# The planned cost of the first loads and of one addition of squares in a self-ordering decoder layer kernel

## The chip, the cores and the metric

One NeuronCore of a Trainium2 chip runs the kernel. Its engines work side by side, each through its own list of instructions in order: TensorE (PE, with its weight loads as PEld), VectorE (DVE), ScalarE (ACT), GpSimd (POOL), and SyncE (SP), which issues most of the DMAs. An instruction that has to wait for another engine or for a load holds everything behind it on its own engine. The metric is the device time of one execution in microseconds (us); less is better.

## The reference

One layer on a sequence of 1024 tokens and 1024 channels, all in f32. Cut to what matters here:

```python
mod = silu(c) @ mod_w + mod_b
shift, scale, gate = split(mod, 3)
h = rmsnorm(x, norm_g) * (1.0 + scale) + shift
u = h @ w_in                       # 5 x 1024 columns: cv, cg, cs, lx, ls
v = cv * sigmoid(cg)               # then a causal convolution of 31 taps,
...                                # LayerNorm, silu, @ pw2_w, times silu(cs)
...                                # lx: short convolution, gates, linear scan, times silu(ls)
x = x + (1.0 + gate) * (concat(conv, lru) @ w_out)
out = rmsnorm(x, final_g)
```

## The kernel before

**Layout.** Everything is kept transposed: channels on the 128 partitions, tokens along the free dimension, in two halves of 512 (`START`). The input x is eight k tiles `x0` to `x7` of 128 x 1024. A product of f32 quality is made of three matmuls in a faster format, from a high part (the value rounded to that format) and a low part (what the rounding left): high x high, high x low, low x high. So every operand of TensorE is first split: ScalarE casts or scales to the high part, VectorE subtracts to the low part.

**The opening.** TensorE should start before the RMS norm and the shift are known. So the first four column tiles (`FIRST`) are computed from x times a scale column alone; the norm's factor per token (`rbc`) and the shift's contribution (`bias`) are applied to the results later. For k tile k this needs:

- the scale column `gs[k]`: a dot product of a 128 x 1024 tile of `mod_w` (`modw8` is for k = 0, `modw9` for k = 1 and so on) with the conditioning row `sc`, on VectorE (`dot`, with an accumulator), and a small operation that makes `gs` from it;
- the high part `uh` and the low part `ul` of x times `gs`, each per half of the tokens: `uh` on ScalarE (the first half of k = 0 on VectorE), `ul` on VectorE;
- the split of the weights, `fhi` on ScalarE and `flo` on VectorE (the names' numbers go by pairs: `flo0` holds k = 0 and 1, `flo2` holds k = 2 and 3);
- 21 matmuls of 512 columns into the banks `first...`: 4 column tiles x 3 terms for the first half and 3 x 3 for the second; the fourth column tile's second half is made up later (`late`).

Beside this run the squares of x (`sq`, ScalarE) and their additions into one tile (VectorE), whose column sums give `rbc`: TensorE sums them (`token_stats`), a small row is written to memory (`rrowd`) and read back as a broadcast to all partitions. Then come the shift's dot products (`modw0` to `modw7`), sums `fsum` of weights times shift, the three slots `NEXT` computed from the same unshifted operands (slots 4 to 6), the `bias` column sums (`psbias`), the gating products `v`, and the operands with the shift in them (`uh`, `ul` written anew) for slot 7 and all that follow.

**What sets the order.** No engine's list is written by hand. Each operation is recorded with an engine, a cost in us, a priority (smaller is sooner) and what it reads and writes. `Plan.order` then plays the whole kernel through with these costs: whenever an engine is free by its model, it takes the ready operation with the smallest priority, and that becomes the engine's order. A load counts as landed when the modelled queue has moved it at its cost. `slack` adds us to the readiness of an operation that hangs on another engine. The real machine then runs these lists in order, with real waits. So a cost in the model moves no time by itself; it moves instructions.

The loads of the opening are recorded in the order of `LOADS`, priority -100, -99, -98 and so on: `s` is the scale's tile of `mod_w`, `a` and `b` the halves of x0, `w` or `W` weights, `x` the later tiles of x, `h` the shift's tiles. The lines that matter are 382 to 385 (`DMA`, the cost of a load), 872 to 878 (the low part and its slack) and 897 to 903 (squares and their additions).

Of the kernel before, what the change touches and what calls it, by code (L numbers as in the profile page):

```python
# [12 lines left out]
ALU = mybir.AluOpType  # L13
# [4 lines left out]
KT = D // P  # L18
# [23 lines left out]
SUM = ("DVE", "DVE", "DVE", "DVE", "DVE", "DVE", "DVE", "DVE")  # L42
# [41 lines left out]
SCALE = ("DVE", "DVE", "DVE", "DVE", "DVE", "DVE", "DVE", "DVE")  # L84
SQP, RSP, BIP, HHP, HCH, EVP = -84, -110, -50, -56, 0.1, -80
RBC_LAG = 2.0


LOADS = "s0 a0 w0 s1 b0 w1 x1 W2 s2 x2 s3 x3 W4 s4 x4 s5 x5 W6 s6 x6 s7 x7 h0 h1 h2 h3 h4 h5 h6 h7".split()
# [205 lines left out]
def hymba_layer(ctx: ExitStack, tc: tile.TileContext, xT, vecs, mod_w, w_first, w_in,  # L295
# [3 lines left out]
    act, dve, pool, pe, sp = nc.scalar, nc.vector, nc.gpsimd, nc.tensor, nc.sync  # L299
# [19 lines left out]
    S = Plan(pools)  # L319
# [41 lines left out]
    def TT(prio, eng, out, a, b, op, n=T, r=(), w=(), reserve=0, after=()):  # L361
        e = dve if eng == "DVE" else pool
        return S.op(eng, d_cost(n) if eng == "DVE" else p_cost(n),
                    lambda: e.tensor_tensor(out=out(), in0=a(), in1=b(), op=op), prio, r, w,  # L364
                    reserve=reserve, lock=not in_psum(r), after=after)
# [14 lines left out]
                    lock=not in_psum(r))  # L380

    def DMA(prio, out, in_, nbytes, r=(), w=(), after=(), reserve=0):
        return S.op("SP", max(0.1, nbytes / 360e3),
                    lambda: sp.dma_start(out(), in_()), prio, r, w, after=after,
                    reserve=reserve)

    def store(prio, eng, out, in_, r, nbytes):
# [359 lines left out]
    for i in range(IDLE):  # L747
        if i == IDLE0:
            for z in (0, 1):
# [3 lines left out]
             after=[spread_op] if i >= IDLE0 else [])  # L753
# [34 lines left out]
    for i, ld in enumerate(LOADS):  # L788
        p = due[ld] = i - 100.0
        k = int(ld[1])  # L790
# [4 lines left out]
        elif ld[0] in "wW":  # L795
# [5 lines left out]
                w=keys(rw))  # L801
            for j in range(k, k + nk):
# [4 lines left out]
                if j:  # L807
                    SUB(p, "DVE", fw_part(lo, j), fw_part(rw, j), fw_part(hi, j), FW,
                        r=[(rw, jj), (hi, jj)], w=[(lo, jj)])
# [31 lines left out]
                    [("a0", 0), ("b1", 0)], [("b1", 0)], lock=True)  # L841

    a0 = ctile("a0", 1)
    begun, uhs, uls, scaled, split_u, last_u = {}, [], [], [], [], {}
    for k in range(KT):
        p = due[f"s{k}"]
        a_ = col(macc, KT + k)
        if k == 0:
            first_dot(p)
        else:  # L850
            dot(SCALE[k], p - 1.5 * (k == 1), KT + k, [gs_op, *(split_u[:1] if k == 1 else [])])
        gs_op = S.op("DVE", 0.2, lambda k=k, a_=a_: dve.scalar_tensor_tensor(
            out=col(gs, k), in0=a_, scalar=col(b1, k), in1=vec("norm_g", k), op0=ALU.add,
            op1=ALU.mult), p, [("macc", KT + k), ("b1", 0)], [("gs", k)], lock=True)
        p = max(p, due[f"x{k}"] if k else p, due[f"w{k}"])
        uh, ul = big_buf(f"uh{k}", F32R, 4), big_buf(f"ul{k}", F32R, 4)
        uhs.append(uh)
        uls.append(ul)
        x_, g = xt[k], gs[:, k:k + 1]
        for a, e in START if k < UK else ((0, T),):  # L860
            n = e - a
            hk = halves(x_, a, e)
            if k == 0 == a:
                o = TS(p, part(uh, a, e), part(x_, a, e), g, None, ALU.mult, n=n,
                       r=hk + [("gs", k)], w=halves(uh, a, e))
            else:
                o = ACT(p, part(uh, a, e), part(x_, a, e), AF.Copy, n, scale=g,
                        r=hk + [("gs", k)], w=halves(uh, a, e))
            if k == 0 == a:
                rw, hi, lo = fw[0]  # L870
                SUB(p, "DVE", fw_part(lo, 0), fw_part(rw, 0), fw_part(hi, 0), FW,
                    r=[(rw, 0), (hi, 0), *halves(uh, a, e)], w=[(lo, 0)])
            split_u.append(STT(
                p, part(ul, a, e), part(x_, a, e), g,
                lambda uh=uh, a=a, e=e: uh()[:, a:e].bitcast(F32), ALU.mult, ALU.subtract, n,
                r=hk + halves(uh, a, e) + [("gs", k)], w=halves(ul, a, e)))
            if k == 0 < a:
                split_u[-1].slack = 1.0
        scaled.append(o)
        for z in range(3 if k == 0 else 0):  # L880
            for i, ps in enumerate(psf):
                o = fw_mm(p, ps, i, uh, ul, k, START[:1], z=z)
                if z == 0:
                    begun[i, 0] = o
                last_u[k, i, 0] = o
        for ch, (a, e) in enumerate(START):
            for i, ps in enumerate(psf):
                if (a, e) not in cuts[i] or k == 0 == a:
                    continue
                q = p + 0.1 * ch if k < LASTK else due[f"w{KT - 1}"] + 0.01 * ((i + 1) % 4) + 0.001 * ch  # L890
                for z in range(3) if k < ZK else (None,):
                    o = fw_mm(q + 0.003 * (z or 0), ps, i, uh, ul, k, ((a, e),),
                              after=[begun[i, a // H]] if k == 0 and a % H else [], z=z)
                last_u[k, i, ch] = o

    sqs = []
    for k in range(KT):
        p = SQP + k
        sq = big_buf(f"sq{k}")
        ACT(p, sq, xt[k], AF.Square, r=[xt[k]], w=[sq], after=[scaled[k]])  # L900
        if k:
            to = sqs[0]
            TT(p, SUM[k], to, to, sq, ALU.add, r=[to, sq], w=[to])
        else:
            sqs.append(sq)
    rbc = big_buf("rbc", parts=4)
# [14 lines left out]
    def turn():  # L921
# [6 lines left out]
        r=[("rrowd", 0)], w=[rbc])  # L928
# [637 lines left out]
```

## Time and profile before

| what | value |
|---|---|
| median of three runs | 732.12 us (731.79 to 732.23) |
| the profiled execution, its own time | 732.15 us |
| its span, first to last instruction | 730.4 us |
| mean granted TensorE clock | 0.997 |

The profile is of one execution. A row of its timeline has the start in us, the duration in us, engine and line, the operation, what it writes `<-` what it reads (without buffer numbers) and how many were merged; in brackets the idle time of the engine just before, and what ended it. A row of the chain has start, duration and what; the chain is followed back from the last instruction to what released each step. A row of a stretch has, for a window of time, the busy time and number of instructions of PE, PEld, DVE, ACT and POOL, the granted clock, the DMA engines' busy share and GB/s. Matmuls overlap in a pipeline, so their rate is read from start to start.

### The profile page before, as it was taken

The numbers are of one execution on the slowest core, as the hardware profiler recorded it, in microseconds if no ns is written. First come the engines' busy times: TensorE is split into PE (matmuls) and PEld (weight loads), VectorE is DVE, ScalarE is ACT, GpSimd is POOL, SyncE is SP. The second block draws the span as 40 slices with busy tenths as digits, with TensorE's granted clock in tenths as the row PEclk, the third lists the DMA queues.
The fourth block names the chain that finished last, engine by engine and source line by source line (L and its number), as shares of the span: only waits on it lengthen the run. The fifth ranks groups of instructions, "written<-read, shape, count | busy, mean of one in ns | idle before, by whom it ended". The sixth has DMA issues, their size and how long they took to land.

```text
span 730.4 us, 8922 instructions
## 1 busy us (share of the span) xinstructions
PE 721.1 (99%) x3270; PEld 599.7 (82%) x3270; DVE 637.5 (87%) x912; ACT 461.1 (63%) x620; POOL 97.9 (13%) x107
## 2 busy tenths in 40 slices
PE   8999999999999999999999999999999999999996
PEld 7888888888888888888888888888888888887885
DVE  6998999999989987688899995998999657899647
ACT  5760585876877977957867896835754334657421
POOL 0034012031222332133121100000000000000001
PEclk9999999999999999999999999999999999999998
DMA  8972023388599799799884536244233430622306
GB/s 321 407 245 90 1 75 91 101 189 200 131 256 238 156 210 212 159 206 213 196 177 90 112 85 190 95 165 165 104 107 115 174 116 0 230 83 92 116 1 230
DMA packets 37499, 112.11 MB, mean 153 GB/s; under 512 B 4168, under 2 KB 12880, under 8 KB 37456
## 3 DMA queue, kind: packets, MB, share of 16 engines
q1 hardware_dynamic: 24048, 76.50, 29.9%
q0 software_dynamic: 12528, 34.26, 26.0%
q10 hardware_dynamic: 880, 0.79, 0.3%
q8 instruction: 25, 0.41, 0.2%
q14 instruction: 18, 0.15, 0.1%
HBM read 64.69 MB, written 12.59 MB: 106 GB/s over the span
## 4 chain that ended last, share of the span: by engine, by line
PE 96%; DVE 2%; DMA 1%; ACT 0%; SPq 0%; issue 0%; DVEq 0%; ACTq 0%
PE ps L495 66%; PE first L775 5%; PE papw L606 3%; PE pbpw L606 3%; PE gate L1197 3%; PE pupw L606 3%; PE puout L606 2%; PE paout L606 2%; PE out L676 2%; PE pcpw L606 1%; PE pb0out L606 1%; PE pcout L606 1%; DVE o L356 1%; DMA x<-in_xT_dram 1%; PE late L775 1%; PE out6b L676 1%
## 5 line engine op out<-in xcount | busy, mean ns | idle before, releaser
L495 PE MATMUL ps<-uh,whi 128*128 128x512 f32 x576 | 224.4, 390 | 0.0
L495 PE MATMUL ps<-uh,wlo 128*128 128x512 f32 x576 | 224.3, 389 | 0.0
L495 PE MATMUL ps<-ul,whi 128*128 128x512 f32 x576 | 224.3, 389 | 0.0
L495 PEld LDWEIGHTS ps<-uh,whi 128*128 128x128 f32 x576 | 108.2, 188 | 22.5
L495 PEld LDWEIGHTS ps<-ul,whi 128*128 128x128 f32 x576 | 108.2, 188 | 22.4
L495 PEld LDWEIGHTS ps<-uh,wlo 128*128 128x128 f32 x576 | 108.1, 188 | 22.3
L337 ACT CAST whi<-raw 128x1024 fp32r<-128x1024 f32 x46 | 48.0, 1047 | 33.9 <-PE ps L495 32.8
L345 ACT ACT_TABLE_LOAD x48 | 61.6, 1283 | 6.2 <-DVE sp8h L378 2.8
L369 POOL DMA_DIRECT2D es<-cq x45 | 40.3, 908 | 156.9 <-ACT cq L345 115.6
L364 DVE TENSOR_TENSOR wlo<-raw,whi 128x1024 fp32r<-128x1024 f32 x39 | 47.5, 1219 | 13.6 <-ACT whi L337 13.6
L356 DVE SCALAR_TENSOR_TENSOR cacc<-v,V,cacc 128x511 f32<-128x511 f32 (+14 forms) x75 | 55.6, 741 | 0.5
L356 DVE SCALAR_TENSOR_TENSOR caccs<-v,V,caccs 128x511 f32<-128x511 f32 (+6 forms) x70 | 52.1, 744 | 2.3 <-ACT caccs L345 1.0
L356 DVE SCALAR_TENSOR_TENSOR caccs<-c,wsum,caccs 128x511 f32<-128x511 f32 (+6 forms) x70 | 52.0, 743 | 0.6
L369 POOL DMA_DIRECT2D oo<-co x42 | 38.3, 913 | 92.1 <-ACT co L345 36.7
L495 PE MATMUL ps<-yh,wlo 128*128 128x512 f32 x128 | 49.8, 389 | 0.0
L495 PE MATMUL ps<-yl,whi 128*128 128x512 f32 x128 | 49.8, 389 | 0.0
L495 PE MATMUL ps<-yh,whi 128*128 128x512 f32 x128 | 49.8, 389 | 0.0
L364 POOL TENSOR_TENSOR o<-fin,bc 128x256 f32<-128x256 f32 x4 | 2.9, 730 | 282.6 <-DMA out_dram<-o 277.5
L356 DVE SCALAR_TENSOR_TENSOR xs<-ps,V,xs 128x512 f32<-128x512 f32 (+3 forms) x48 | 35.8, 745 | 0.2
L345 ACT ACTIVATE cq<-v,V 128x511 f32<-128x511 f32 (+14 forms) x45 | 31.9, 708 | 0.0
L364 POOL TENSOR_TENSOR wlo<-raw,whi 128x1024 fp32r<-128x1024 f32 x7 | 18.2, 2627 | 88.8 <-ACT whi L337 88.8
L356 DVE SCALAR_TENSOR_TENSOR modw<-modw,sc 128x1024 f32<-128x1024 f32 x23 | 30.1, 1313 | 0.0
(380 smaller groups left out, 1455.7 us busy)
## 6 DMA issues: line engine op xcount, KB each, us to landing
raw<-in_w_in_dram SPq DMA_DIRECT2D x36, 512.0 KB, 5.2
modw<-in_mod_w_dram SPq DMA_DIRECT2D x24, 512.0 KB, 8.6
raw<-in_w_out_dram SPq DMA_DIRECT2D x10, 512.0 KB, 3.9
scsd<-scs SPq DMA_DIRECT2D x8, 512.0 KB, 4.3
acc<-in_xT_dram SPq DMA_DIRECT2D x8, 512.0 KB, 4.2
accd<-acc SPq DMA_DIRECT2D x8, 512.0 KB, 2.7
rawpw<-in_pw_dram SPq DMA_DIRECT2D x8, 512.0 KB, 3.4
scsr<-scsd SPq DMA_DIRECT2D x8, 512.0 KB, 5.4
```

The costliest lines, as they stand in the source:

```text
L337: act.copy(out(), in_())
L345: act.activation(out=out(), in_=in_(), func=func, **kw)
L356: dve.scalar_tensor_tensor(out=out(), in0=in0(), scalar=scalar, in1=in1(), op0=op0, op1=op1, accum_out=accum)
L364: lambda: e.tensor_tensor(out=out(), in0=a(), in1=b(), op=op), prio, r, w,
L369: return S.op("POOL", ISSUE, lambda: pool.dma_start(out(), a(), accum_op=ALU.add), prio, r, w, lag=RATE * n / T, after=after)
L495: pe.matmul(part(ps, a - off, b - off)(), k3(lhs)()[:, k, :], rhs[k]()[:, a:b], start=(k == 0 and lhs is wh and rhs is xh and (a - off) % ...
L606: pe.matmul(part(ps, 0, c1 - c0)(), half(*lhs)()[:, j * P:j * P + P], half(*rhs)()[:, c0:c1], start=start and j == 0 and z == 0, stop=j == ...
L676: pe.matmul(part(ps, a - off, e - off)(), k3(lhs)()[:, k, :], rhs()[:, i * H + a % H:i * H + a % H + e - a], start=k == KORD[0] and lhs is ...
L775: pe.matmul(part(ps, a - off, b - off)(), fw_part(lhs, k, i * P, i * P + P)(), rhs()[:, a:b], start=k == 0 and lhs is wh and rhs is xh, st ...
L1197: pe.matmul(ps(), lhs()[:, j, :], rhs()[:, c0:c1], start=st == 0, stop=st == 2)
```

## The change

Four numbers of the plan and one dependence. Loads of the opening are costed at 410 thousand bytes per us instead of 360 thousand (those with a priority below -68.1, which are all of `LOADS`); the second and third load, the first half of x0 and the weights of k = 0, get costs of their own, 2.27 and 1.2 us; the slack of the low part of k = 0's second half goes from 1.0 to 0.5 us; and the addition of tile 1's squares waits for the low part of tile 2.

```diff
+FIRSTCOST, EARLYRATE, SQD, SQK, ULS = {-99: 2.27, -98: 1.2}, 410e3, 1, 1, 0.5
...
     def DMA(prio, out, in_, nbytes, r=(), w=(), after=(), reserve=0):
-        return S.op("SP", max(0.1, nbytes / 360e3),
-                    lambda: sp.dma_start(out(), in_()), prio, r, w, after=after,
+        cost = max(0.1, nbytes / (EARLYRATE if prio < -94.5 + KT * 3.3 else 360e3))
+        cost = FIRSTCOST.get(round(prio), cost) if prio < -96 else cost
+        return S.op("SP", cost, lambda: sp.dma_start(out(), in_()), prio, r, w, after=after,
                     reserve=reserve)
...
-    begun, uhs, uls, scaled, split_u, last_u = {}, [], [], [], [], {}
+    begun, uhs, uls, scaled, split_u, last_u, last_split = {}, [], [], [], [], {}, []
...
             if k == 0 < a:
-                split_u[-1].slack = 1.0
+                split_u[-1].slack = ULS
         scaled.append(o)
+        last_split.append(split_u[-1])
...
             to = sqs[0]
-            TT(p, SUM[k], to, to, sq, ALU.add, r=[to, sq], w=[to])
+            TT(p, SUM[k], to, to, sq, ALU.add, r=[to, sq], w=[to],
+               after=[last_split[k + SQD]] if k <= SQK else [])
```

What it does to the lists shows at three places. The numbers in the names are those of buffers.

**VectorE, k tiles 0 and 1.** Before, from the first high part on (`ul0` is the low part of k = 0, `modw9` the dot product for k = 1):

```order
L378 TENSOR_SCALAR uh0_170<-x0_125,gs_90 128x512
L364 TENSOR_TENSOR flo0_176<-fraw0_140,fhi0_155 128x512
L356 SCALAR_TENSOR_TENSOR ul0_186<-x0_125,gs_90,uh0_170 128x512
L364 TENSOR_TENSOR flo0_176<-fraw0_140,fhi0_155 128x512
L356 SCALAR_TENSOR_TENSOR modw9_142,macc_93<-modw9_142,sc_152 128x1024
L356 SCALAR_TENSOR_TENSOR ul0_186<-x0_125,gs_90,uh0_170 128x512
L852 SCALAR_TENSOR_TENSOR gs_90<-macc_93,b1_94,V_77 128x1
L364 TENSOR_TENSOR flo2_223<-fraw2_166,fhi2_215 128x512
L356 SCALAR_TENSOR_TENSOR ul1_229<-x1_159,gs_90,uh1_220 128x512 x2
```

And now:

```order
L379 TENSOR_SCALAR uh0_164<-x0_125,gs_90 128x512
L357 SCALAR_TENSOR_TENSOR ul0_173<-x0_125,gs_90,uh0_164 128x512
L365 TENSOR_TENSOR flo0_181<-fraw0_132,fhi0_167 128x512
L357 SCALAR_TENSOR_TENSOR modw9_148,macc_93<-modw9_148,sc_151 128x1024
L854 SCALAR_TENSOR_TENSOR gs_90<-macc_93,b1_94,V_77 128x1
L357 SCALAR_TENSOR_TENSOR ul0_173<-x0_125,gs_90,uh0_164 128x512
L365 TENSOR_TENSOR flo0_181<-fraw0_132,fhi0_167 128x512
L357 SCALAR_TENSOR_TENSOR ul1_220<-x1_171,gs_90,uh1_211 128x512 x2
```

The dot product and the scale column of k = 1 and the second low part of k = 0 stand ahead of the low weights of k = 1 (the second `flo0`); the first low part stands ahead of the low weights of k = 0; the low weights of k = 2 went behind the low parts of k = 1. On ScalarE the second copy of the row `sc` went ahead of the cast `fhi0` of k = 0, and the high parts of k = 1 ahead of the cast of k = 2's weights.

**VectorE, k tiles 2 and 3.** Before, from tile 2's dot product (`modw10`) on:

```order
L356 SCALAR_TENSOR_TENSOR modw10_182,macc_93<-modw10_182,sc_152 128x1024
L364 TENSOR_TENSOR flo2_223<-fraw2_166,fhi2_215 128x512
L852 SCALAR_TENSOR_TENSOR gs_90<-macc_93,b1_94,V_77 128x1
L364 TENSOR_TENSOR sq0_192<-sq0_192,sq1_239 128x1024
L356 SCALAR_TENSOR_TENSOR ul2_269<-x2_200,gs_90,uh2_260 128x512 x2
L356 SCALAR_TENSOR_TENSOR modw11_212,macc_93<-modw11_212,sc_152 128x1024
L364 TENSOR_TENSOR flo4_291<-fraw4_244,fhi4_284 128x512
L852 SCALAR_TENSOR_TENSOR gs_90<-macc_93,b1_94,V_77 128x1
```

And now:

```order
L357 SCALAR_TENSOR_TENSOR modw10_191,macc_93<-modw10_191,sc_151 128x1024
L365 TENSOR_TENSOR flo2_234<-fraw2_179,fhi2_224 128x512
L854 SCALAR_TENSOR_TENSOR gs_90<-macc_93,b1_94,V_77 128x1
L357 SCALAR_TENSOR_TENSOR modw11_218,macc_93<-modw11_218,sc_151 128x1024
L357 SCALAR_TENSOR_TENSOR ul2_269<-x2_204,gs_90,uh2_257 128x512 x2
L854 SCALAR_TENSOR_TENSOR gs_90<-macc_93,b1_94,V_77 128x1
L365 TENSOR_TENSOR sq0_199<-sq0_199,sq1_237 128x1024
L365 TENSOR_TENSOR flo4_296<-fraw4_245,fhi4_283 128x512
```

The dot product of tile 3 (`modw11`) stands ahead of tile 2's low parts (`ul2`), the addition of squares behind them.

**SP and ScalarE, around the broadcast of the row statistics.** SP's loads before:

```order
L384 DMA raw8_499<-in_w_in_dram 128x1024
L384 DMA raw6_502<-in_w_in_dram 128x1024
L384 DMA graw1_518<-in_gate_w_dram 128x256
L384 DMA rbc_528<-rrowd_101 128x1024
L384 DMA modw6_564<-in_mod_w_dram 128x1024
```

And now:

```order
L386 DMA raw8_478<-in_w_in_dram 128x1024
L386 DMA graw1_490<-in_gate_w_dram 128x256
L386 DMA modw5_516<-in_mod_w_dram 128x1024
L386 DMA rbc_539<-rrowd_101 128x1024
L386 DMA modw6_566<-in_mod_w_dram 128x1024
```

The load of `modw5` (the shift's sixth tile) went from ahead of the slots' weights to just ahead of the broadcast load. On ScalarE, whose list issues the write of the small row, stood before:

```order
L345 ACTIVATE st_100<-token_stats_121,eps_t_88 128x8
L337 CAST whi4_512<-raw4_455 128x1024
L345 ACTIVATE fsum_486<-raw5_465,shift_91 128x128
L337 COPY rbc_528<-token_stats_121 8x128
L337 CAST ghi0_530<-graw0_477 128x256
L926 DMA rrowd_101<-rbc_528 8x128
```

And now:

```order
L346 ACTIVATE st_100<-token_stats_121,eps_t_88 128x8
L338 CAST whi4_521<-raw4_430 128x1024
L338 CAST whi7_529<-raw7_469 128x1024
L338 COPY rbc_539<-token_stats_121 8x128
L338 CAST whi8_541<-raw8_478 128x1024
L930 DMA rrowd_101<-rbc_539 8x128
```

Two casts of whole weight tiles stand where two smaller operations stood. Among TensorE's matmuls the bias sums (`psbias`) went 18 matmuls back, from inside slot 6 to the beginning of slot 7, and the sums of the squares (`token_stats`) 3 matmuls back. From about a quarter of each list on, the orders of before and now are equal, apart from buffer numbers.

## The prediction

> **What bounds the kernel now.** I read the page first (busy shares), then the waits of TensorE, then the engines' busy time by stretch, and last the opening instruction by instruction. Of the page:
>
> ```profile
> PE 721.1 (99%) x3270; PEld 599.7 (82%) x3270; DVE 637.5 (87%) x912; ACT 461.1 (63%) x620; POOL 97.9 (13%) x107
> ```
>
> TensorE is busy for 99% of the span, so an edit to the order pays only where TensorE stands still. The view of its waits names those places (total us, times, longest):
>
> ```profile
> PE first L775 <- DVE ul L356: 0.8, 1, 0.8
> PE puout L606 <- ACT eout L337: 0.7, 1, 0.7
> ```
>
> The second lies near 661 us. The first is in the opening, as this stretch shows (us of each engine, then clock, DMA share, GB/s):
>
> ```profile
> 10.00:15.00 5.00, 4.25 (x19) 2.95 (x18) 3.62 (x7) 3.88 (x6) 0.00 (x0) 1.00 1.03 420
> ```
>
> TensorE (first) has holes there, and VectorE (third) 1.4 us of idle time. The timeline shows the holes, and the chain the undisturbed pace (start, us, what):
>
> ```profile
> 8.62 1.19 PE L775 MATMUL first<-uh,fhi 128*128 128x512 f32 x4 [0.22 <-ACT fhi L337]
> 9.65 1.08 PE L775 MATMUL first<-uh,flo 128*128 128x512 f32 x4
> 13.75 0.98 PE L775 MATMUL first<-ul,fhi 128*128 128x512 f32 x3 [0.75 <-DVE ul L356]
> 14.64 1.20 PE L775 MATMUL first<-uh,fhi 128*128 128x512 f32 x4
> 15.67 1.08 PE L775 MATMUL first<-uh,flo 128*128 128x512 f32 x4
> 24.75 0.46 PE L775 MATMUL first<-ul,fhi 128*128 128x512 f32 x1
> 25.05 0.40 PE L775 MATMUL first<-uh,fhi 128*128 128x512 f32 x1
> 47.82 2.96 PE first L775 x12
> 56.21 29.92 PE ps L495 x132
> ```
>
> The pace is 29.92 / 132 = 0.227 us for a 512-column matmul. A k tile has 21 of them (4 column tiles of the first half and 3 of the second, three terms each): 4.76 us. Tile 0 begins at 8.62 and tile 1 at 14.64. The first four from 8.62 take until 9.65, 1.03 instead of 0.91, so a start from rest costs 0.12. Without a hole tile 1 would start at 8.62 + 4.76 + 0.12 = 13.50. **Lost there: 1.14.** Tile 1 starts from rest again (14.64 to 15.67, 1.03): **0.12**. At 24.75 the low part of tile 3 comes just in time, and from it to the next matmul are 0.30: **0.07**. All that an opening can give back at these places is 1.14 + 0.12 + 0.07 = 1.33.
>
> **Why the hole is there.** VectorE and ScalarE in the same stretch, and the landings that they need (for tile 1's scale weights, its x and tile 3's scale weights the issue, then us from issue to landing):
>
> ```profile
> 8.60 0.69 DVE L364 TENSOR_TENSOR flo<-fraw,fhi 128x512 fp32r<-128x512 f32 x1 [0.70 <-ACT fhi L337]
> 9.21 0.75 DVE L356 SCALAR_TENSOR_TENSOR ul<-x,gs,uh 128x512 fp32r<-128x512 f32 x1
> 11.19 0.69 DVE L364 TENSOR_TENSOR flo<-fraw,fhi 128x512 fp32r<-128x512 f32 x1 [1.24 <-ACT fhi L337]
> 11.80 1.22 DVE L356 SCALAR_TENSOR_TENSOR modw<-modw,sc 128x1024 f32<-128x1024 f32 x1
> 12.95 0.75 DVE L356 SCALAR_TENSOR_TENSOR ul<-x,gs,uh 128x512 fp32r<-128x512 f32 x1
> 13.61 0.21 DVE L852 SCALAR_TENSOR_TENSOR gs<-macc,b,V 128x1 f32<-128x1 f32 x1
> 14.62 1.41 DVE L356 SCALAR_TENSOR_TENSOR ul<-x,gs,uh 128x512 fp32r<-128x512 f32 x2 [0.19 <-ACT uh L345]
> 9.93 0.72 ACT L345 ACTIVATE uh<-x,gs 128x512 fp32r<-128x512 f32 x1 [0.87 <-DMA x<-in_xT_dram]
> 10.56 0.60 ACT L337 CAST fhi<-fraw 128x512 fp32r<-128x512 f32 x1
> 11.07 1.05 ACT L345 ACTIVATE sq<-x 128x1024 f32<-128x1024 f32 x1
> 13.86 1.34 ACT L345 ACTIVATE uh<-x,gs 128x512 fp32r<-128x512 f32 x2 [0.15 <-DVE gs L852]
> L384 SPq DMA_DIRECT2D modw<-in_mod_w_dram x1: 432/432/432, 2.6 to 2.6; - x1
> DMA to landing us min/median/max: 6.6/6.6/6.6
> L384 SPq DMA_DIRECT2D x<-in_xT_dram x1: 710/710/710, 4.0 to 4.0; - x1
> DMA to landing us min/median/max: 7.8/7.8/7.8
> L384 SPq DMA_DIRECT2D modw<-in_mod_w_dram x1: 328/328/328, 7.9 to 7.9; - x1
> DMA to landing us min/median/max: 9.0/9.0/9.0
> ```
>
> VectorE works in order. After the low part of tile 0's first half (9.21) the next in its queue is tile 1's low weights, whose cast ends at 11.16: it stands 1.24 us, while the scale weights of tile 1 have been there since 2.6 + 6.6 = 9.2 and the high part of x0's second half since 10.65. Both stand behind the waiting instruction, and TensorE behind them.
>
> **The change, part by part.** It alters planned costs only, so nothing is added or removed; what counts is the new order. I go through it with the durations above; on VectorE an independent successor starts about 0.08 before the end (8.60 + 0.69 against 9.21), a dependent one 0.04 to 0.05 after it.
>
> *Tile 0.* The first low part goes ahead of tile 0's low weights, into the 0.70 that VectorE waited for the cast (7.90 to 8.60); being 0.75 long it hardly delays the low weights, which run 8.62 to 9.31, and TensorE wants them at 9.65. Free. The second copy of the conditioning row goes ahead of that cast on ScalarE, into time in which it waited for the load: free; if it were late it would cost its 0.58, as it would then hold the cast and the first matmul.
>
> *Tile 1.* The dot product with the scale weights starts at 9.23 (landed 9.2) and ends at 10.45; the scale column is ready at 10.70; the low part of the second half follows, 10.71 to 11.46, and TensorE wants it at 8.62 + 0.12 + 18 x 0.227 = 12.83: 1.4 early. Tile 1's low weights run 11.37 to 12.06. ScalarE ends the squares at 12.12 and then, with the column there and x1 landed at 4.0 + 7.8 = 11.8, makes tile 1's high parts, 12.07 to 13.41; the first is done at 12.79, and TensorE wants it at 13.50: 0.7 early. Low parts 12.83 to 14.24, wanted from 13.50 + 8 x 0.227 = 15.32. So tile 1 can start at 13.50.
>
> *Tile 2.* Low weights, dot product and low weights of tile 3 run 14.16 to 16.5, the column is there at 16.7, the high part at 17.5; wanted at 13.50 + 4.76 = 18.26: 0.7 early. Now the dot product for tile 3 stands ahead of tile 2's low parts, and it waits for its weights, landed 7.9 + 9.0 = 16.9. Behind it queue those low parts: 18.10 to 18.85 for the first, wanted at 18.26 + 1.82 = 20.08: 1.2 early. If that load were later by more than 1.2, every further us would be TensorE's.
>
> *Tile 3.* One addition of squares (1.22, by the equal dot product) now stands behind tile 2's low parts instead of ahead of them. Column, addition and low weights put tile 3's low parts at 21.3; the first is done at 22.05, wanted at 18.26 + 4.76 + 0.45 = 23.47. The narrow place at 24.75 gets 1.4 of cover. Later tiles gain more, as VectorE stays some 0.8 ahead of its old times while landings stay as they were: the loads' order on SP is unchanged up to the eighth x tile, and DMA is full at 420 GB/s either way.
>
> So 1.33 comes back. What of it is kept? TensorE then has no hole until 661 us, so all later work moves up by this much, if the rest keeps pace. From about 165 us on the orders of before and after are equal, so the 0.7 near 661 and the end stay as they are.
>
> *Further on.* The load that broadcasts the row statistics stands one 512 KB load further back on SP, and two casts of 1.05 stand ahead of it on ScalarE. VectorE waits for it at 54 us, has idle time again between 60 and 70, and is then full until TensorE's slot 7 takes its low parts one by one, from 90 us on (columns of the stretches as above; the cast is a group of the page):
>
> ```profile
> L337 ACT CAST whi<-raw 128x1024 fp32r<-128x1024 f32 x46 | 48.0, 1047 | 33.9 <-PE ps L495 32.8
> 54.05 3.68 DVE L364 TENSOR_TENSOR first_u<-first,rbc 128x512 f32<-128x512 f32 x6 [1.75 <-DMA rbc<-rrowd]
> 60.00:65.00 5.00, 5.00 (x24) 4.15 (x23) 3.31 (x8) 0.00 (x0) 2.11 (x1) 1.00 0.32 105
> 65.00:70.00 5.00, 5.00 (x24) 4.14 (x23) 4.17 (x13) 0.00 (x0) 0.11 (x1) 1.00 0.00 0
> 80.00:85.00 5.00, 5.00 (x24) 4.15 (x23) 5.00 (x11) 3.08 (x6) 0.00 (x0) 1.00 0.00 0
> ```
>
> So VectorE can fall back by 1.69 + 0.83 = 2.5 against TensorE at no cost. The inserted load takes between 1.25 (512 KB at the 420 GB/s of the opening) and a whole flight of 6.6, the casts between 0 and 2.1 (they replace two smaller operations): together 1.25 to 8.7. I take 1.25 + 1.05 = 2.3, near the lower end because queued loads followed each other at that rate in the opening. That is just covered: zero.
>
> The bias sums move 18 matmuls back among TensorE's work, and sigmoids and the gating products `v` hang on them:
>
> ```profile
> 87.62 0.17 ACT L337 COPY bias<-psbias 128x7 f32<-128x7 f32 x1 [0.73 <-PE psbias L962]
> 89.73 2.19 ACT L345 ACTIVATE first_u<-first_u,bias 128x1024 f32<-128x1024 f32 x2
> 91.19 2.91 DVE L356 SCALAR_TENSOR_TENSOR v<-first_u,bias,first_u 128x512 f32<-128x512 f32 x4
> ```
>
> The copy comes at 87.62 + 18 x 0.227 - 1.33 = 90.4. An activation between it and the sigmoids is gone, so the first of these starts some 1.4 later instead of 2.1 and ends at 92.9. VectorE has three more operations of 0.66 ahead of the first product and reaches it between 91.19 + 2.0 - 1.33 = 91.9 and, if it gains nothing, 93.2. It waits 0 to 1.0 there, and low parts queue behind; by the 2.3 above it is at the later end, so again zero.
>
> Sum: 732.15 (the profiled execution's own time: span 730.4 and 1.75 around it) - 1.33 = 730.8. That execution is 0.03 above the median of the three runs, 732.12.
>
> **The rivals.** *The broadcast holds VectorE (slower).* If the inserted load delays the broadcast by a whole flight, VectorE falls back by 6.6, 2.5 of it is covered, and TensorE waits 4.1 in slot 7: 732.15 - 1.33 + 4.1 = 734.9; with the casts in full on top, 737.0. It decides from 2.5 on, and from 3.8 on the kernel is slower than before. For it: VectorE is full from 70 us on, and my value is close to the cover. Against: loads in the opening stood behind each other in the queue (flights of 6.6 to 9.0) and still came at 420 GB/s. With both casts in full and the load at 1.3 it would be 3.4, less 2.5: 0.9 lost, 731.7.
>
> *The end loses it to the clock.* The end is sparse; a stretch and a piece of the chain:
>
> ```profile
> 722.00:725.00 3.00, 2.08 (x16) 1.70 (x15) 2.20 (x8) 0.63 (x2) 0.32 (x1) 1.00 0.67 221
> 722.98 0.72 PE finbc L705 x4
> ```
>
> The granted clock is still 1.00 with 2.08 busy of 3. If work that comes 1.33 sooner met a half clock, this piece would double: 730.8 + 0.7 = 731.5. [...] The three executions of before lie within 0.44 (731.79 to 732.23), so a 0.7 of this kind is rare.
>
> *The cover in the opening is thinner.* Tile 1's and tile 2's high parts have 0.7 each. Were they late by 0.7 more than that, half of the gain would go: 731.5.
>
> *More than the sum.* In the chain the 12 matmuls from 47.82 took 2.96 instead of 2.72, a start from rest after the row statistics that is not in my sum. If it went too, with such a term or two more, it would be 0.3 to 0.5: 730.4.
>
> *The change does nothing here.* If the wait only moved to the next load, the result would be 732.1. Against it: the load that matters landed at 9.2, 2.6 before VectorE used it.
>
> **How the numbers follow.** 0.2% of 732.12 is 1.46, about what a measurement of this kernel can tell from no change, so faster means under 730.66; my 730.8 lies close above that. Forecast, 730.5 to 731.1: 0.68, of it 0.32 under the bound, since the sum can miss by 0.2 either way. More than the sum: 0.14, all of it faster. Part lost in the opening, at the broadcast or to the clock, 731.1 to 732: 0.09. Nothing: 0.02. The broadcast holds VectorE: 0.07, all of it slower by over 0.2%. That makes faster 0.46, same 0.47, slower 0.07. The range 730.2 to 732.1 leaves out the slower case and a still larger gain.
>
> **What would show it.** Right: tile 1's matmuls start at 13.4 to 13.7, VectorE's dot product at 9.2, no wait of TensorE on `ul` in the view of waits, that of 0.7 near 661 still there, the end 1.3 sooner. Wrong: a wait of TensorE on a high part near 13.5 or 18.3, on a low part between 85 and 103 us, with VectorE waiting longer for `rbc` or for `first_u`, or a granted clock below 1.00 before 720 us.

## The result and the profile after

| | before | changed |
|---|---|---|
| median of 22 executions each | 732.01 us (731.58 to 732.71) | 730.78 us (730.13 to 731.23) |
| span of the profiled execution | 730.4 us | 729.1 us |
| mean granted clock in it | 0.997 | 0.999 |

The ratio of the changed kernel to the one before is 0.9982, with a 95% interval of 0.9976 to 0.9989: 0.18% faster, 1.23 us by the medians. The forecast was 730.8.

Busy times in the changed kernel (page), and the longest of TensorE's waits after its first matmul (view of waits):

```profile
PE 720.9 (99%) x3270; PEld 600.2 (82%) x3270; DVE 638.9 (88%) x912; ACT 460.1 (63%) x619; POOL 97.4 (13%) x107
```

```profile
PE puout L608 <- ACT eout L338: 0.7, 1, 0.7
```

The engines do nearly the same work as before: ScalarE has one table load less (47 instead of 48), and the busy times differ by at most 1.4. What went is one row: the wait on `ul` of 0.8. That of 0.7 near 660 stays. The stretch in which TensorE had 0.75 of idle time is full:

```profile
10.00:15.00 5.00, 5.00 (x23) 4.09 (x22) 4.50 (x9) 5.00 (x8) 0.00 (x0) 1.00 1.03 420
```

The opening in the timeline, and further on the first row of the chain after it:

```profile
8.67 1.20 PE L777 MATMUL first<-uh,fhi 128*128 128x512 f32 x4
9.70 1.21 PE L777 MATMUL first<-uh,flo 128*128 128x512 f32 x4
13.72 1.07 PE L777 MATMUL first<-uh,fhi 128*128 128x512 f32 x4
14.62 1.07 PE L777 MATMUL first<-uh,flo 128*128 128x512 f32 x4
18.48 1.07 PE L777 MATMUL first<-uh,fhi 128*128 128x512 f32 x4
7.51 0.59 ACT L338 COPY sc<-c_row 128x512 f32<-128x512 f32 x1 [1.12 <-DVE modw L357]
7.99 0.62 ACT L338 CAST fhi<-fraw 128x512 fp32r<-128x512 f32 x1
7.51 0.22 DVE L854 SCALAR_TENSOR_TENSOR gs<-macc,b,V 128x1 f32<-128x1 f32 x1
8.29 0.75 DVE L357 SCALAR_TENSOR_TENSOR ul<-x,gs,uh 128x512 fp32r<-128x512 f32 x1
8.96 0.68 DVE L365 TENSOR_TENSOR flo<-fraw,fhi 128x512 fp32r<-128x512 f32 x1
9.56 1.22 DVE L357 SCALAR_TENSOR_TENSOR modw<-modw,sc 128x1024 f32<-128x1024 f32 x1
55.02 34.00 PE ps L497 x150
```

Tile 1 starts at 13.72 instead of 14.64, without a start from rest (0.90 to its next group instead of 1.03), tile 2 at 18.48 instead of 19.54. The slots start at 55.02 instead of 56.21: 1.19 of the gain is there by the end of the opening, and nothing is added or lost after it. (The piece has 150 matmuls instead of 132, since the bias sums went 18 back.)

### The profile page after: what moved, and what is told of

It is laid out like the page before. It is cut to its first block, busy times and chain, and to the rows that moved or that the text cites. A ratio compares the mean times of both kernels' runs of the same rounds, so it can differ in the third digit from the quotient of the medians.

```text
span 729.1 us, 8918 instructions
## 1 busy us (share of the span) xinstructions
PE 720.9 (99%) x3270; PEld 600.2 (82%) x3270; DVE 638.9 (88%) x912; ACT 460.1 (63%) x619; POOL 97.4 (13%) x107
## 4 chain that ended last, share of the span: by engine, by line
PE 98%; DVE 1%; ACT 0%; issue 0%; DVEq 0%
PE ps L497 66%; PE first L777 5%; PE pbpw L608 3%; PE pupw L608 3%; PE papw L608 3%; PE gate L1201 3%; PE puout L608 2%; PE paout L608 2%; PE out L678 2%; PE pcpw L608 1%; PE pb0out L608 1%; PE pcout L608 1%; DVE o L357 1%; PE out6b L678 1%; PE late L777 1%; PE token_stats L743 1%
## 5 line engine op out<-in xcount | busy, mean ns | idle before, releaser
L346 ACT ACTIVATE cq<-c,wsum 128x512 f32<-128x512 f32 x42 | 29.6, 713 | 0.0
```

The costliest lines, as they stand in the source:

```text
L346: act.activation(out=out(), in_=in_(), func=func, **kw)
```

## The experiments

In some runs the planner's lists are edited by hand after planning: `S.moves` takes pairs, and the operations of the first part are put, on their own engine, ahead of the operation in the second. All other lists stay as planned. `dots[1]` is the dot product for k = 1, `gsop[1]` its scale column, `ulop[k, a]` and `uhop[k, a]` the low and high part of tile k from column a, `subs[k]` and `casts[k]` the split of tile k's weights.

### VectorE's order in tile 1, undone alone

```diff
+    S.moves.append(([subs[1]], dots[1]))
```

> The changed kernel with one move on VectorE alone: the low weights of k = 1 go back ahead of that tile's dot product; every other list is as in the changed kernel. If the whole gain is the instruction that VectorE stood at, the hole comes back in full: VectorE waits about 0.6 for the cast, the dot product starts near 11.8, the second low part of tile 0 ends near 14.0, tile 1 starts at 14.5 to 14.7, one wait of TensorE on ul of 1.0 to 1.3, and the time is 730.8 + 1.25 = 732.0. If the gain comes from the other moves (ScalarE's order, the squares, later tiles), little returns: 730.8 to 731.1.

Measured: 732.34 us, ratio 1.0005 (0.9996 to 1.0014). The whole gain is gone with one move. VectorE's two rows and TensorE's in the timeline:

```profile
10.97 0.69 DVE L389 TENSOR_TENSOR flo<-fraw,fhi 128x512 fp32r<-128x512 f32 x1 [1.24 <-ACT fhi L362]
11.58 1.22 DVE L381 SCALAR_TENSOR_TENSOR modw<-modw,sc 128x1024 f32<-128x1024 f32 x1
13.78 0.98 PE L801 MATMUL first<-ul,fhi 128*128 128x512 f32 x3 [0.52 <-DVE ul L381]
14.59 1.09 PE L801 MATMUL first<-uh,fhi 128*128 128x512 f32 x4
```

VectorE stands 1.24 for the cast, twice the 0.6 that was expected, with the dot product behind it, and tile 1 starts at 14.59. TensorE's wait is 0.5, where 1.0 to 1.3 was expected: tile 0 itself began later here (8.76). In this execution the slots start at 55.93, so the trace shows 0.9 of the 1.19 given back. That this instruction stands where it does is necessary for the gain. Whether it is enough is the next question.

### The same order alone, in the kernel before

```diff
+    S.moves.append(([dots[1], gsop[1], ulop[0, 512]], subs[1]))
```

> The kernel before with one move on VectorE alone: dot product, scale column of k = 1 and second low part of tile 0 go ahead of the low weights of k = 1. If that order is the whole cause, tile 1 starts at 13.5 and the time is 732.0 - 1.2 = 730.8. The rival: ScalarE still casts the weights of k = 2 (landed 13.06) ahead of tile 1's high parts, so these end near 14.4 instead of 12.8, TensorE waits 0.9 to 1.0 on uh in place of ul, and the time is 731.8.

Measured: 731.87 us, ratio 1.0000 (0.9991 to 1.0009): the rival. TensorE and ScalarE:

```profile
12.97 0.62 ACT L361 CAST fhi<-fraw 128x512 fp32r<-128x512 f32 x1 [0.96 <-DMA fraw<-in_w_first_dram]
13.49 1.33 ACT L369 ACTIVATE uh<-x,gs 128x512 fp32r<-128x512 f32 x2
14.27 1.20 PE L799 MATMUL first<-uh,fhi 128*128 128x512 f32 x4 [0.69 <-ACT uh L369]
```

The low part is in time, and the wait went over to the high part: ScalarE stood 0.96 for a load that nobody needed yet, with tile 1's high parts behind it.

### With ScalarE's order as well

```diff
+    S.moves.append(([dots[1], gsop[1], ulop[0, 512]], subs[1]))
+    S.moves.append(([uhop[1, 0], uhop[1, 512]], casts[2]))
```

> The kernel before with the move on VectorE and, on ScalarE, tile 1's high parts ahead of the cast of k = 2's weights; no load is costed anew, the squares and the later tiles stay in their old order. By the sum of the prediction, which gave 1.14 + 0.12 of 1.33 to tile 1, the time is 730.8 to 730.9. The rival: the later tiles in their old order have cover for tile 1's old start only, and TensorE, 1.2 sooner there, meets the same loads: waits of 0.3 near 18 (high part of tile 2) and 0.7 to 0.8 near 24 (low part of tile 3), 1.1 of 1.2 given back, 731.9.

Measured: 731.70 us, ratio 0.9998 (0.9989 to 1.0007): the rival again, though tile 1 now starts where the prediction wants it.

```profile
13.47 1.07 PE L799 MATMUL first<-uh,fhi 128*128 128x512 f32 x4
15.45 1.20 PE L799 MATMUL first<-ul,fhi 128*128 128x512 f32 x4
18.75 1.20 PE L799 MATMUL first<-uh,fhi 128*128 128x512 f32 x4
24.75 0.50 PE L799 MATMUL first<-ul,fhi 128*128 128x512 f32 x1 [0.47 <-DVE ul L380]
14.04 0.69 DVE L388 TENSOR_TENSOR flo<-fraw,fhi 128x512 fp32r<-128x512 f32 x1 [1.85 <-ACT fhi L361]
14.65 1.41 DVE L380 SCALAR_TENSOR_TENSOR ul<-x,gs,uh 128x512 fp32r<-128x512 f32 x2
```

Before, the last of these four TensorE rows also began at 24.75. So 1.17 won at tile 1 is given back in three pieces by the low part of tile 3, without one long wait anywhere. The first row of VectorE shows the reason for the first piece: it stands 1.85 for the cast of k = 2's weights, with tile 1's low parts queued behind it. Whether the other two follow from it is what the next run asks.

### And a third move

```diff
+    S.moves.append(([ulop[1, 0], ulop[1, 512]], subs[2]))
```

> The kernel before with three moves by hand: the two of the run before (dot product, scale column and second low part ahead of the low weights of k = 1 on VectorE; tile 1's high parts ahead of the cast of k = 2's weights on ScalarE), and a third, tile 1's low parts ahead of the low weights of k = 2 on VectorE. Loads are costed as before and the squares stay where they were. If the low parts of tile 1 that stood behind a cast were what gave the gain back, the waits at 15.4, 18.7 and 24.7 go, tile 1 starts at 13.4 to 13.7 and tile 2 at 18.2 to 18.5, and the time is 730.8. The rival: tile 3 stays narrow as long as its dot product stands behind tile 2's low parts and the squares ahead of them; then 0.5 to 0.8 of wait stays near 24 and the time is 731.4 to 731.7.

Measured: 731.00 us, ratio 0.9982 (0.9973 to 0.9990): the changed kernel's ratio, with three moves by hand and nothing else of the change. A wait of 0.3 is left at tile 3 (23.32) in an execution whose first matmul came at 7.91, 0.7 sooner than in the profile of before, because its weights had landed sooner. So these three places are enough for the gain, within what the times can tell. That VectorE's order and the third move are needed is shown by the runs without them; that ScalarE's is needed was not run with the other two in place, and rests on the wait of 0.69 on `uh` above.

### The parts of the change

The costs of the loads alone (changed kernel, slack and squares as before):

```diff
-FIRSTCOST, EARLYRATE, SQD, SQK, ULS = {-99: 2.27, -98: 1.2}, 410e3, 1, 1, 0.5
+FIRSTCOST, EARLYRATE, SQD, SQK, ULS = {-99: 2.27, -98: 1.2}, 410e3, 1, 0, 1.0
```

> The changed kernel with the new costs of the loads alone: slack 1.0 as before, and no dependence of the squares. VectorE's lists of tiles 0 and 1 are as in the changed kernel but for the second low part of tile 0, which stands behind the low weights of k = 1; in tile 2 the squares stand ahead of its low parts and tile 3's dot product behind them, as before. If the costs of the loads do the work and the other two parts only add cover, 730.8 with no wait of TensorE between 9 and 40. If tile 3 needs the dependence (the prediction gave 0.07 to it), 730.9 to 731.0; if tile 0's second low part now comes late, a wait near 13 and up to 731.4.

Measured: 730.87 us, ratio 0.9984 (0.9975 to 0.9992), and no wait of TensorE in the opening. The other two parts, each alone with the old costs (`{}, 360e3`): first the slack,

> The kernel before with one part of the change alone, the slack of 0.5: on VectorE the second low part of tile 0 follows the first, ahead of the dot product and the low weights of k = 1; ScalarE's list stays. The low part that TensorE waited for is then ready near 11.5, but the scale column of k = 1 still stands behind the low weights and tile 1's high parts behind the cast of k = 2's weights. By the run with VectorE's order alone the wait goes over to uh: 0.7 to 1.0 near 14.3, 731.8. If the low part was all, 730.9.

Measured: 731.76 us, ratio 0.9995 (0.9986 to 1.0004), and the wait where it was expected:

```profile
14.38 1.19 PE L777 MATMUL first<-uh,fhi 128*128 128x512 f32 x4 [0.77 <-ACT uh L346]
```

then the squares:

> The kernel before with one part of the change alone, the dependence of the squares: tile 3's dot product stands ahead of tile 2's low parts and the addition behind them, tiles 0 and 1 are as before. The hole at tile 1 stays, as it was (0.75 of wait on ul), and only the narrow place at 24.75 can go: 732.0 less 0.07, 731.9 to 732.0. If the squares had a share of their own in the gain, 731.5 or less.

Measured: 731.92 us, ratio 1.0000 (0.9991 to 1.0008), with the hole in place (0.86 on `ul`). The costs of the loads give the gain; the other two parts give none that can be measured, alone or on top.

### What VectorE can be late by, further on

Four, then eight operations without effect, put on VectorE behind the first product with `rbc`:

```diff
+                    for _ in range(4):
+                        dve.tensor_tensor(out=rbc()[:, :H], in0=rbc()[:, :H],
+                                          in1=rbc()[:, :H], op=ALU.max)
```

> The changed kernel with four operations of 0.61 that change nothing (the larger of the broadcast row and itself, 128 x 512) put on VectorE behind the first product with the broadcast row, near 55: VectorE is 2.4 later. By the cover of 2.5 that the prediction worked out, nothing is lost: 730.8. By the idle time that the trace of the changed kernel has left between 60 and 70 (0.17 + 0.94 = 1.1), TensorE waits for 1.3 near 88: 732.1.

> As the run before with eight such operations: VectorE is 4.9 later. By a cover of 2.5: 730.8 + 2.4 = 733.2. By a cover of 1.1: 730.8 + 3.8 = 734.6, with the wait in slot 7, near 88. This is also the size of the slower rival, which had the broadcast 6.6 late and 4.1 lost.

Measured: 738.92 us and 741.76 us, ratios 1.0095 (1.0080 to 1.0110) and 1.0132 (1.0118 to 1.0145). Neither theory had this; all four expected numbers fell, for two reasons that the trace of the run with four shows. Timeline, then stretches (of TensorE alone: busy, clock, DMA share, GB/s):

```profile
52.00 7.55 POOL L365 TENSOR_TENSOR wlo<-raw,whi 128x1024 fp32r<-128x1024 f32 x3
55.09 6.46 DVE L1305 TENSOR_TENSOR rbc<-rbc 128x512 f32<-128x512 f32 x4
86.92 0.39 PE L497 MATMUL ps<-uh,whi 128*128 128x512 f32 x1
88.15 0.50 PE L497 MATMUL ps<-ul,whi 128*128 128x512 f32 x1 [0.84 <-DVE ul L357]
88.73 0.40 PE L497 MATMUL ps<-uh,whi 128*128 128x512 f32 x1
91.86 0.80 PE L497 MATMUL ps<-ul,whi 128*128 128x512 f32 x1 [2.73 <-DVE ul L357]
```

```profile
90.00:91.00 1.00, 0.00 (x0) 0.89 0.02 8
91.00:92.00 1.00, 0.14 (x1) 0.50 0.00 0
...
100.00:101.00 1.00, 1.00 (x4) 0.50 0.00 0
101.00:102.00 1.00, 1.00 (x6) 0.99 0.00 0
```

First, the four took 6.46 instead of the 2.44 that was reckoned: until 59.55 GpSimd's subtractions ran beside them, and from there to the end are 2.0. So VectorE was 6.5 late, not 2.4. TensorE's gaps are 88.15 - 87.15 = 1.0 and 91.86 - 88.96 = 2.9, together 3.9. The cover is thus 6.5 - 3.9 = 2.6. Second, behind the gaps the granted clock stood at a half from 90.8 to 101.0. The kernel lost 8.1; the gaps are 3.9 of it, and the other 4.2 is about what the half clock takes (9.1 us from the end of the gaps to 101.0, with 0.43 from one matmul to the next instead of 0.23). In the run with eight, TensorE's two gaps are 3.4 and 2.3, and from 92.36 until 104.2 its 512-column matmuls in a row are 0.43 apart, too.

The first product itself reads a PSUM bank, and in the changed kernel it had its usual 0.61 to the next one (55.06 to 55.67) with GpSimd's subtractions beside it (49.30 to 59.77). So it was repeated instead:

```diff
+                o.emit = lambda emit=o.emit: [emit() for _ in range(6)]
```

> The changed kernel with the first product with the broadcast row, the one of the late bank near 55, done six times over in a row instead of once: 5 x 0.61 = 3.1 of VectorE's time, read from a bank, so that GpSimd's work beside it does not slow it as it did the operations in the two runs before. With the cover of 2.6 that those gave (6.5 late, 3.9 of it TensorE's), TensorE waits 0.5 in slot 7; by the idle time in the trace of the changed kernel (1.1), 2.0. The clock is the second question. If any wait of TensorE there brings the half clock, as the 1.0 and 2.9 did, 3 to 4 more are lost: 734 to 737. If the clock falls only behind a long gap, the wait is all there is: 731.3 to 732.8 with the granted clock at 1.00 from 85 to 105.

```profile
55.16 4.32 DVE L365 TENSOR_TENSOR first_u<-late,rbc 128x512 f32<-128x512 f32 x6 [5.00 <-PE late L777]
59.39 1.28 DVE L365 TENSOR_TENSOR first_u<-first,rbc 128x512 f32<-128x512 f32 x2
88.28 0.39 PE L497 MATMUL ps<-uh,whi 128*128 128x512 f32 x1
89.66 0.50 PE L497 MATMUL ps<-ul,whi 128*128 128x512 f32 x1 [1.00 <-DVE ul L357]
90.24 1.62 PE L966 MATMUL psbias<-ones,fsum 128*128 128x1 f32 x14
```

VectorE is 59.39 - 55.16 - 0.61 = 3.6 late (0.72 each instead of 0.61), TensorE's gap is 89.66 - 88.51 = 1.15, so the cover is 2.5. The median is 732.88 us, ratio 1.0013 (1.0003 to 1.0022), but the twelve times fall into two groups of six: 731.45 to 732.14, with a mean granted clock of 0.999, about what the gap alone would give, and 733.62 to 735.06, with 0.993 to 0.997. The profiled execution, with a span of 732.3, is one of the second kind, and shows a half clock for one piece of 3.4 (92.1 to 95.5):

```profile
91.00:92.00 1.00, 1.00 (x9) 1.00 0.00 0
92.00:93.00 1.00, 1.00 (x4) 0.56 0.00 0
...
95.00:96.00 1.00, 1.00 (x5) 0.74 0.00 0
```

So both answers to the second question hold, by chance of the execution.

### What the opening still has

The low weights of k = 0 ahead of the first low part, as before:

```diff
+    S.moves.append(([subs[0]], ulop[0, 0]))
```

> The changed kernel with one move on VectorE: the low weights of k = 0 ahead of the first low part, as before. The prediction called the new order free; the trace of the changed kernel has the low weights ready at 9.64 and TensorE's second group at 9.70 with a start from rest. If that is where the missing 0.1 to 0.2 at tile 1 is, the second group starts at 9.65 without a wait, tile 1 at 13.5, and the time is 730.6. If it is not, or if the conditioning row comes in time by itself, 730.8. Either is within what the timing can tell; the trace decides.

Measured: 730.96 us, ratio 0.9984 (0.9975 to 0.9993). It settles nothing: in the profiled execution the scale column came early and the weights late (cast at 8.22), so the order made no difference. Then the same with the cast in two pieces:

```diff
-                ACT(p, fw_part(hi, j), fw_part(rw, j), "copy", FW, r=[(rw, jj)], w=[(hi, jj)])
+                    ACT(p - 0.01, fw_part(hi, j, 0, P), fw_part(rw, j, 0, P), "copy", P,
+                        r=[(rw, jj)], w=[(hi, 9)])
+                    ACT(p, fw_part(hi, j, P), fw_part(rw, j, P), "copy", FW - P,
+                        r=[(rw, jj), (hi, 9)], w=[(hi, jj)])
```

> The changed kernel with the two moves that its opening still has room for: the low weights of k = 0 ahead of the first low part, and the cast of k = 0's weights in two pieces, 128 columns first, so that TensorE's first matmul waits for 0.25 of cast instead of 0.62. If TensorE's start is set by that cast, the first matmul starts about 0.3 sooner after the landing of the weights; the low weights of k = 0 end as late as before, so 0.1 to 0.3 of it stays: 730.5 to 730.7. If the first high part of x or the landing is what TensorE waits for, nothing: 730.8 to 731.0.

```profile
8.35 0.71 ACT L362 CAST fhi<-fraw 128x128 fp32r<-128x128 f32 x2 [1.19 <-DMA fraw<-in_w_first_dram]
8.70 1.38 PE L801 MATMUL first<-uh,fhi 128*128 128x512 f32 x4 [0.89 <-ACT fhi L362]
13.80 1.07 PE L801 MATMUL first<-uh,fhi 128*128 128x512 f32 x4
```

The first matmul starts 0.35 behind the cast's start (0.68 in the changed kernel: 7.99 to 8.67), and tile 1 5.45 behind it (5.73 there). Measured: 730.64 us, ratio 0.9982 (0.9974 to 0.9991). It has the lowest median of all, 0.14 under the changed kernel, which this measurement cannot tell from nothing.

## Why the prediction was right, point by point

**The cause.** Right, and shown: VectorE in order, standing at the low weights of k = 1. Put back alone, that instruction takes the whole gain by the times, and 0.9 of 1.19 by the trace of one execution.

**The sum.** 1.33 was forecast; the chain has 1.19 at 55 and 1.2 before the last pieces, the medians 1.23. The restart (0.12) and the narrow place at 24.75 (0.07) went as said. The largest term, 1.14 at tile 1, is 0.92 between the two profiled executions. Taken from the first matmul to tile 1, which leaves out when the weights land, the stretch is:

| kernel | first matmul to tile 1, us |
|---|---|
| before | 14.64 - 8.62 = 6.02 |
| VectorE's order undone | 14.59 - 8.76 = 5.83 |
| VectorE's order alone | 14.27 - 8.53 = 5.74 |
| both orders | 13.47 - 8.59 = 4.88 |
| three moves | 12.81 - 7.91 = 4.90 |
| costs of the loads alone | 13.78 - 8.88 = 4.90 |
| changed | 13.72 - 8.67 = 5.05 |

The prediction had 4.88. The changed kernel's 5.05 contains a step that it called free: the first low part ahead of the low weights of k = 0. In this execution the scale column came 0.35 later than in the profile of before (7.51 against 7.16), so the low part held the low weights until 9.64. TensorE loads weights ahead of its matmuls (the load for the group at 10.74 starts at 10.51), and this load waited:

```profile
9.70 0.77 PEld L777 LDWEIGHTS first<-uh,flo 128*128 128x128 f32 x4 [0.27 <-DVE flo L365]
```

The second group took 1.04 (9.70 to 10.74) instead of 0.91. Free was right only for the times of the one execution that the prediction had. The run with the move undone, which has this order too, shows the same wait of 0.27 (at 9.78); the one with the costs of the loads alone shows none (weight load at 9.72, matmul at 9.89).

A second step that was called free cost something too: the copy of the conditioning row ahead of the cast on ScalarE. The prediction had named what would happen if the row were late, and it was: the copy starts at 7.51, and the cast right behind it at 7.99. The weights had landed by about 7.9 (2.10 + 5.8), so here it is 0.1; in the execution of the run with the move undone the copy starts at 7.60 and the cast at 8.08.

**Why the sum is kept.** The prediction counted the later tiles' new order as cover and named margins for it. The runs show that this was half of the matter: with tile 1 repaired alone, the gain is lost by tile 3. Its margins for tiles 1 and 2 were right because it worked them out from the new lists, with tile 1's high and low parts ahead of k = 2's split. Its tile 3 step was right in sign, but the moved squares that it rests on are not needed: without them there was no wait either.

**The broadcast.** The step was wrong and cost nothing. It had the broadcast 2.3 later, behind one more load and two casts. SP and VectorE in the changed kernel (for the load of `rbc`, issue and flight):

```profile
45.51 0.33 SPq L386 DMA_DIRECT2D modw<-in_mod_w_dram  x1
49.13 0.33 SPq L386 DMA_DIRECT2D rbc<-rrowd  x1
DMA to landing us min/median/max: 4.4/4.4/4.4
55.06 0.69 DVE L365 TENSOR_TENSOR first_u<-late,rbc 128x512 f32<-128x512 f32 x1 [2.34 <-PE late L777]
```

The load ahead of it was issued 3.6 sooner, while SP had nothing to do but wait for the small row. It took 3.3 and had landed by 48.8, before the load of `rbc` was issued, so it delayed nothing. `rbc` landed at 53.5, 0.4 sooner than before. VectorE then waited for the bank `late` instead, whose product had moved to the front, and began its products 1.0 later than before (55.06 against 54.05) for a reason that the prediction did not have. That the zero of this step held is luck.

**The cover of 2.5.** The number came out, 2.6 and 2.5 by the two experiments, but not for the reason given. The prediction read it as VectorE's idle time between 60 and 70 in the kernel before. The experiments measured the changed kernel, which has 1.1 of idle time left there. Another 0.8 is the margin of the low part that TensorE takes behind the second gap: in the changed kernel it ends at 87.57 and its matmul starts at 88.41. Where the rest comes from was not followed up, so the agreement is partly luck.

**Slot 7** was right: the copy of the bias was forecast for 90.4 and the first sigmoid's end for 92.9. It ends at 93.1, and VectorE's first product `v` starts at 93.25, with no wait of TensorE behind it.

```profile
90.51 0.17 ACT L338 COPY bias<-psbias 128x7 f32<-128x7 f32 x1 [0.38 <-PE psbias L966]
91.99 2.20 ACT L346 ACTIVATE first_u<-first_u,bias 128x1024 f32<-128x1024 f32 x2
```

**The rivals.** The slower one did not come, but its price was too small: VectorE 6.6 late was put at a wait of 4.1 and 734.9. The run with 6.5 late had gaps of 3.9, as priced, and 738.9, since the clock was left out. Its threshold, slower than before from 3.8 late, was too mild too: at 3.6 late six of twelve executions are 1.6 or more above the median of before. The end did not meet a half clock (722 to 725 has 1.00), and no run shows that a mere shift of work brings one: where TensorE worked at half clock, gaps of its own stood ahead (1.15; 1.0 and 2.9; 3.4 and 2.3). The thin cover in the opening was not touched: tile 1's and tile 2's first high parts are done about 1.0 ahead of TensorE. Nor did more than the sum come back: behind the row statistics nine matmuls take 2.28 instead of 2.04, the same start from rest of 0.24 as before.

## What to carry to other kernels

When a wait of the busiest engine is to be removed, list what stands next in line at the same place, on every engine that feeds it: here neither one move nor two gave a gain that can be told from nothing, and only the third let it through. Where a planner sets the order, costs of the loads nearer to the measured rate (410 in the plan, 420 GB/s in the trace, where it had been 360) made all three moves at once. And price a gap of TensorE with the clock behind it, not only with its own length: in the run with four operations the gaps are 3.9 of the 8.1 lost.

## What the hardware showed that was not expected

**The clock after short gaps.** In the profiled execution of the repeated product a gap of 1.15, with 1.5 of one-column matmuls soon behind it (90.24 to 91.72), was followed by 3.4 us at half clock (92.1 to 95.5), and six of its twelve times are about 2 us longer than the other six. Gaps of 1.0 and 2.9 brought 10.2 us at half clock (90.8 to 101.0). With gaps of 3.4 and 2.3 the matmuls came at 0.43 until 104.2, the pace that the run with four has at a granted clock of 0.50. The opening's gap in the kernel before, 0.9 (12.83 to 13.75), brought none: the clock is 1.00 from 10 to 18. What decides whether the clock falls, and for how long, the runs do not show.

**VectorE beside GpSimd.** The four operations with both inputs in SBUF took 6.46, 4.5 of it until GpSimd's subtractions ended at 59.55 and 2.0 after that. Other operations with both inputs in SBUF were longer beside these subtractions too. In the changed kernel, where they end at 59.77, the product of `first_u` with `rbc` at 59.25 took 1.08; in the run with four it came at 65.18, with GpSimd at rest, and took 0.68. A dot product took 3.43 (47.01 in the changed kernel) where the usual one takes 1.22. The products with one input in PSUM kept their pace beside the same work: in the changed kernel six took 3.67 from 55.67 on, 0.61 each. The cause of the difference was not shown.

**The start moves.** In the nine profiled executions read for it (before, changed, the move undone, VectorE's order alone, both orders, three moves, the costs of the loads alone, and the two of the opening) the cast of k = 0's weights began between 7.24 and 8.35, and TensorE's first matmul between 7.91 and 8.89. In six the cast followed the landing of the weights; in the other three, all with the new order on ScalarE, it followed the copy of the conditioning row (7.99, 8.08 and 8.02). One execution's end thus says little about a tenth of a us; the stretch from the first matmul to tile 1 lies between 4.88 and 4.90 in the three runs of the table where nothing held it.
